# Eight start distances for the squared activations of a two-layer MLP

## The chip, the cores and the metric

The kernel runs on one core of a Trainium2 chip. The metric is the device time of one launch in microseconds: before the change the median of three runs is 565.23 us (563.58 to 565.45).

## The reference, cut to what matters

The program is a trunk of two decoder layers over 256 tokens of width 1024, all in fp32. Each layer has a token mixer with a memory cross-attention beside it, and then an MLP. The change touches only the MLP:

```python
D_MODEL, SEQ, DEPTH, D_FF = 1024, 256, 2, 4096

for i in range(DEPTH):
    # pooling mixer (layer 0) or block attention (layer 1), memory attention, w_out
    x = x + jnp.concatenate([tok, mo], axis=-1) @ w_out[i]
    u = rms_norm(x, g_mlp[i])
    x = x + jnp.square(jax.nn.relu(u @ w_ff1[i])) @ w_ff2[i]
return x
```

## The kernel before, in words

Every matrix product is made in a shortened fp32 form. An operand is split into a high part `hi` and a remainder `lo` (`split`, L105 to L115; ScalarE makes `hi`, VectorE makes `lo`), and a product is the sum of hi by hi, hi by lo and lo by hi. `mm3` (L117 to L120) issues these three multiplies into one PSUM tile. In a multiply TensorE holds one operand of 128 rows by 128 columns still (the weight load, PEld in the profile) and streams the other past it.

The MLP works in eight groups of 512 hidden features (`mlp`, L391 to L471).

- `ff1(g)` computes the group's hidden values. Here the split weights stand still, in pieces of 128 columns, and the transposed residual stream (`x1T`, in layer 1 `x3T`) is streamed: L418 streams 512 columns (high and low part side by side), L420 streams 256. The first group works in four accumulators and alternates four multiplies of L418 with four of L420; the other groups run eight and eight.
- `square` (L394 to L405) takes the result out of PSUM, applies the squared ReLU, and writes the split result: ScalarE writes `hh` at L404, VectorE writes `hl` at L405. Two such pairs a group hold four blocks of 128 features by 256 tokens.
- `ff2(g)` multiplies them into four accumulators. Here `hh` and `hl` stand still, in slices of 128 columns, and the split weights `hi` and `lo`, which came from HBM a moment ago, are streamed with 512 columns. That is 48 multiplies a group, 384 a layer, 768 in all.

The groups are interleaved: `ff1(g)` is issued, then `ff2(g - 1)`. The order on TensorE is the order of the code. All weights arrive over SyncE's DMA queue (L100).

Where a tile lies in SBUF is set by its pool. The pools of the weights (`rawp`, `wp`) and of the transposed activations (`tp`) hold tiles of whole multiples of 512 bytes a partition; in the program as built they all begin at 32 modulo 512. The pool `m0` of the first MLP and `m1` of the second, with `hh` and `hl`, begin behind the pool `mkp`, in which a tile that nothing uses takes 96 floats:

```python
    mkp.tile([P, 96], F32, tag="gap", name="gap")
```

With it `hh`, `hl` and the other tiles of `m0` and `m1` begin at 32 modulo 512 too. A slice of 128 fp32 columns is 512 bytes. So the start of a standing slice in `ff2` lies a whole multiple of 512 bytes from the start of the streamed weights. The same holds for `ff1`, `w_out` and the input projections.

Two places of layer 0 differ. The buffers `hhi` and `hlo` of the pooling stage follow a tile of 2304 bytes (`bw1`, L523), which is four and a half times 512, so they begin at 288. The band multiplies (L564, L565) hold slices of `hhi` and `hlo` and stream `bw0`, which begins at 32: a distance of 256. The keys of the memory attention of layer 0 (`mkh`, `mkl`, streamed) also begin at 288 and the queries (`mqh`, `mql`, standing) at 32; in layer 1 both begin at 32.

Of the kernel before, what the change touches and what calls it, by code (L numbers as in the profile page):

```python
# [11 lines left out]
F32R = mybir.dt.float32r  # L12
# [6 lines left out]
P = 128  # L19
# [14 lines left out]
QG, KG = 58, 122  # L34
NSMALL = 186
NWARM = 8
LAG = 2

PLAN = {'x': 6, 'q': 5, 'bw': 7, 'pool': 5, 'mem0': (1, 3, 6, 6),
# [14 lines left out]
def trunk(ctx: ExitStack, tc: tile.TileContext, x, mem, x_t, mem_t, small, bands, rope, mask,  # L54
# [13 lines left out]
    def nm(s):  # L68
        uid[0] += 1
        return f"{s}_{uid[0]}"  # L70

    def psum(name="ps"):
        return psp.tile([P, 512], F32, tag="ps", name=nm(name))

    def accum():
        return accp.tile([P, 512], F32, tag="acc", name=nm("acc"))
# [12 lines left out]
    wps = psum("warm")  # L89
    for _ in range(NWARM):  # L90
        nc.tensor.matmul(wps, warm[:, :P], warm, start=True, stop=True)
# [3 lines left out]
    def load_raw(src):  # L95

        n = src.shape[1]
        k = src.shape[0] // P
        r = rawp.tile([P, k, n], F32, tag="raw", name=nm("raw"))
        nc.sync.dma_start(r, src.rearrange("(k p) n -> p k n", p=P))  # L100
        return r
# [3 lines left out]
    def split(raw, g=None):  # L105
        n = raw.shape[-1]
        hi = wp.tile([P, n], F32R, tag="hi", name=nm("hi"))
        lo = wp.tile([P, n], F32R, tag="lo", name=nm("lo"))
        if g is None:
            nc.scalar.activation(hi, raw, AF.Copy)  # L110
            nc.vector.tensor_tensor(lo, raw, hi.bitcast(F32), op=ALU.subtract)  # L111
        else:
            last_hi[0] = nc.scalar.activation(hi, raw, AF.Copy, scale=g)  # L113
            nc.vector.scalar_tensor_tensor(lo, raw, g, hi.bitcast(F32), op0=ALU.mult, op1=ALU.subtract)  # L114
        return hi, lo  # L115

    def mm3(o, a, b, start, stop):  # L117
        nc.tensor.matmul(o, a[0], b[0], start=start, stop=False)  # L118
        nc.tensor.matmul(o, a[0], b[1], start=False, stop=False)  # L119
        nc.tensor.matmul(o, a[1], b[0], start=False, stop=stop)  # L120
# [20 lines left out]
    def big_t(name):  # L141

        t = tp.tile([P, NKC, 2, S], F32R, tag="t", name=nm(name))
        return t[:, :, 0, :], t[:, :, 1, :], t
# [125 lines left out]
    def later(fn):  # L270
        pend.append(fn)
        while len(pend) > LAG:
            pend.pop(0)()
# [108 lines left out]
    def mlp_stats():  # L382
        e2 = []
        for b in range(2):
            ms = norm_stats(xr[:, b, :], f"mlp{b}")
            r2 = st.tile([P, 1], F32, tag=f"r2{b}", name=nm("r2"))
            nc.vector.reciprocal(r2, ms)
            e2.append(r2)
        return e2

    def mlp(l, t, hp, finish):  # L391
        acc = []

        def square(zs, hh, hl):  # L394

            z = hp.tile([P, 2, S], F32, tag="r", name=nm("r"), bufs=2)
            for i in range(2):
                c = hp.tile([P, S], F32, tag="c", name=nm("c"), bufs=2)
                nc.scalar.activation(c, zs[i][:, S:], AF.Copy)  # L399
                nc.vector.tensor_tensor(z[:, i, :], zs[i][:, :S], c, op=ALU.add)  # L400
            z = z.rearrange("p i t -> p (i t)")
            h = hp.tile([P, 512], F32, tag="h", name=nm("h"), bufs=2)
            nc.vector.scalar_tensor_tensor(h, z, 0.0, z, op0=ALU.max, op1=ALU.mult)
            nc.scalar.activation(hh, h, AF.Copy)  # L404
            nc.vector.tensor_tensor(hl, h, hh.bitcast(F32), op=ALU.subtract)  # L405

        def ff1(g):
            pieces = []
            for q in range(4):
                raw = load_raw(w_ff1[l][q * 256:(q + 1) * 256, g * 512:(g + 1) * 512])  # L410
                for j in range(2):
                    k = 2 * q + j
                    pieces.append(split(raw[:, j, :], sm[:, GMLP + 8 * l + k:GMLP + 8 * l + k + 1]))

            def steps(o, n, ks):

                for k in ks:
                    nc.tensor.matmul(o, pieces[k][0][:, n * P:(n + 1) * P], t[2][:, k, :, :], start=k == 0, stop=False)  # L418
                for k in ks:
                    nc.tensor.matmul(o[:, :S], pieces[k][1][:, n * P:(n + 1) * P], t[0][:, k, :],  # L420
                                     start=False, stop=k == NKC - 1)

            res = [(hp.tile([P, 512], F32R, tag="hh", name=nm("hh"), bufs=4),
                    hp.tile([P, 512], F32R, tag="hl", name=nm("hl"), bufs=4)) for _ in range(2)]
            if g == 0:
                z = [accum() for _ in range(4)]
                for k0 in (0, 4):
                    for n in range(4):
                        steps(z[n], n, range(k0, k0 + 4))
                for i in range(2):  # L430
                    square(z[2 * i:2 * i + 2], *res[i])
                return res
            for i in range(2):
                z = [psum("step") for _ in range(2)]
                for n in range(2):
                    steps(z[n], 2 * i + n, range(NKC))
                square(z, *res[i])
            return res

        def ff2(g, hs):  # L440
            last = g == 7
            if g == 0:
                acc.extend([[accum(), accum()], [accum(), accum()]])
            held = []

            def go(b, h, f, pieces):
                hh, hl = hs[f // 2]
                o = (f % 2) * S + b * P
                mm3(acc[b][h], (hh[:, o:o + P], hl[:, o:o + P]), pieces[h], g == 0 and f == 0, last and f == 3)

            for f in range(4):
                raw = load_raw(w_ff2[l][g * 512 + f * P:g * 512 + (f + 1) * P, :])
                held.append([split(raw[:, 0, h * 512:(h + 1) * 512]) for h in range(2)])
                if not last:
                    for b in range(2):
                        for h in range(2):
                            go(b, h, f, held[f])
            if last:
                for h in range(2):
                    for b in range(2):  # L460
                        for f in range(4):
                            go(b, h, f, held[f])
                        finish(b, h, acc[b][h])

        prev = ff1(0)
        r2.extend(mlp_stats())
        for g in range(1, 8):
            cur = ff1(g)
            ff2(g - 1, prev)
            prev = cur  # L470
        ff2(7, prev)  # L471
# [11 lines left out]
    with tc.tile_pool(name="l0", bufs=1) as lp:  # L483
# [74 lines left out]
        dhi, dlo, _ = big_t("d")  # L558
# [59 lines left out]
        for l in range(2):  # L618
            g = cp.tile([P, 1], F32, tag=f"mg{l}", name=f"mg{l}")
# [45 lines left out]
    with tc.tile_pool(name="l1", bufs=1) as lp:  # L665
# [6 lines left out]
        for i, (gc, f) in enumerate(((QG, 1.0), (KG, 8.0))):  # L672
            for b in range(2):
                cc, ss = rp[:, b, 0, :], rp[:, b, 1, :]
                g1, g2 = sm[:, gc:gc + 32], sm[:, gc + 32:gc + 64]
                for j, (g, src, sg) in enumerate(((g1, cc, f), (g2, cc, f), (g2, ss, -f), (g1, ss, f))):
                    nc.vector.scalar_tensor_tensor(tcs[:, b, j // 2, i, (j % 2) * 32:(j % 2) * 32 + 32],
                                                   g, sg, src, op0=ALU.mult, op1=ALU.mult)
# [185 lines left out]
```

## Time and profile before

| | |
|---|---|
| median of three runs | 565.23 us (563.58 to 565.45) |
| profiled execution | 565.1 us, its span 563.3 us |
| TensorE (PE) busy | 554.2 us, 98% of the span |
| weight loads (PEld) busy | 459.6 us, 82% |
| VectorE (DVE) busy | 397.3 us, 71% |
| ScalarE (ACT) busy | 343.3 us, 61% |
| granted TensorE clock | 0.997 of full speed |
| moved by DMA | 101.94 MB, mean 181 GB/s |

The span reaches from the first to the last instruction. Multiplies are pipelined: the recorded duration of one reaches from its start until its last results are out, so that consecutive ones overlap, and what each takes of TensorE's time is read from the start of one to the start of the next. In the lists of groups a mean duration stands behind the busy time.

### The profile page before, as it was taken

The page shows a single profiled execution, that of the slowest core. Times are in us where ns is not written, and L with a number is a line of the kernel's source. Part 1 is how long each engine was busy: PE and PEld are TensorE (multiplying, and loading weights), DVE is VectorE, ACT ScalarE, POOL GpSimd, SP SyncE. Part 2 cuts the span into 40 slices and gives each one's busy share as a digit, 9 for nine tenths or more (in the row PEclk, how much of TensorE's full clock was granted, in tenths as well). Part 3 has the DMA queues.
Part 4 walks back from the last instruction along what each step waited for, and adds up shares of the span by engine and source line. Part 5 has one row for each costly group of instructions (what it writes and reads, how often), then busy time and mean ns, then how long its engine had stood idle before and what let it go on. Part 6 is the DMA issues. An engine that isn't in the chain of part 4 may idle for free.

```text
span 563.3 us, 8161 instructions
## 1 busy us (share of the span) xinstructions
PE 554.2 (98%) x2884; PEld 459.6 (82%) x2884; DVE 397.3 (71%) x793; ACT 343.3 (61%) x659; POOL 24.4 (4%) x27
## 2 busy tenths in 40 slices
PE   7999999999999999999999999999999999999997
PEld 3888788888888888888887777878888888888885
DVE  4798986775855856847879999667768477486542
ACT  5789976663763754745766887656647456466330
POOL 0111110000000000000012112000000000000000
PEclk9999999999999999999999999999999999999999
DMA  8979855546637548448563333455374483573301
GB/s 262 339 274 317 260 182 163 161 138 224 207 135 257 166 149 284 124 175 274 152 217 119 113 118 115 143 159 176 107 269 139 161 287 106 205 229 138 121 0 74
DMA packets 46696, 101.94 MB, mean 181 GB/s; under 512 B 3648, under 2 KB 11584, under 8 KB 46656
## 3 DMA queue, kind: packets, MB, share of 16 engines
q1 hardware_dynamic: 46656, 101.43, 54.9%
q8 instruction: 22, 0.36, 0.3%
q14 instruction: 18, 0.15, 0.1%
HBM read 100.37 MB, written 1.05 MB: 180 GB/s over the span
## 4 chain that ended last, share of the span: by engine, by line
PE 90%; DVE 3%; ACT 2%; DMA 1%; POOL 1%; issue 1%; SPq 0%; DVEq 0%; ACTq 0%
PE step L418 18%; PE acc L119 18%; PE acc L120 17%; PE acc L118 17%; PE step L420 9%; PE acc L418 3%; PE av_out L334 1%; PE acc L420 1%; DMA raw<-in_w_in_pool_dram 1%; PE exp_t L298 1%; POOL r L164 1%; PE transpose L137 1%; DVE lo L114 1%; PE tok_scores L714 1%; ACT hi L113 1%
## 5 line engine op out<-in xcount | busy, mean ns | idle before, releaser
L114 DVE SCALAR_TENSOR_TENSOR lo<-raw,sm,hi 128x512 fp32r<-128x512 f32 x212 | 150.5, 745 | 33.1 <-ACT hi L113 19.6
L113 ACT ACTIVATE hi<-raw,sm 128x512 fp32r<-128x512 f32 x212 | 140.8, 717 | 33.0 <-PE acc L120 29.9
L110 ACT ACTIVATE hi<-raw 128x512 fp32r<-128x512 f32 (+1 forms) x152 | 92.0, 626 | 46.1 <-PE acc L120 40.7
L111 DVE TENSOR_TENSOR lo<-raw,hi 128x512 fp32r<-128x512 f32 (+1 forms) x152 | 97.0, 682 | 19.7 <-ACT hi L110 19.7
L118 PE MATMUL acc<-hi,hh 128*128 128x512 f32 x256 | 99.9, 390 | 0.0
L119 PE MATMUL acc<-lo,hh 128*128 128x512 f32 x256 | 99.8, 390 | 0.0
L120 PE MATMUL acc<-hi,hl 128*128 128x512 f32 x256 | 99.8, 390 | 0.0
L400 DVE TENSOR_TENSOR r<-step,c 128x256 f32<-128x256 f32 x56 | 23.6, 422 | 57.8 <-ACT c L399 57.8
L399 ACT ACTIVATE c<-step 128x256 f32<-128x256 f32 x56 | 21.3, 380 | 68.8 <-PE step L420 68.8
L120 PEld LDWEIGHTS acc<-hi,hl 128*128 128x128 f32 x256 | 48.1, 188 | 10.1
L418 PE MATMUL step<-x1T,hi 128*128 128x512 f32 x224 | 55.9, 392 | 0.0
L418 PE MATMUL step<-x3T,hi 128*128 128x512 f32 x224 | 55.9, 392 | 0.0
L118 PEld LDWEIGHTS acc<-hi,hh 128*128 128x128 f32 x256 | 48.1, 188 | 9.5
L119 PEld LDWEIGHTS acc<-lo,hh 128*128 128x128 f32 x256 | 48.1, 188 | 9.4
L418 PEld LDWEIGHTS step<-x3T,hi 128*128 128x128 f32 x224 | 40.7, 189 | 7.5
L418 PEld LDWEIGHTS step<-x1T,hi 128*128 128x128 f32 x224 | 40.6, 189 | 7.5
L420 PEld LDWEIGHTS step<-x3T,lo 128*128 128x128 f32 x224 | 30.6, 190 | 2.2
L420 PEld LDWEIGHTS step<-x1T,lo 128*128 128x128 f32 x224 | 30.6, 190 | 2.2
L118 PE MATMUL acc<-hi,x2T 128*128 128x512 f32 x80 | 32.1, 401 | 0.0
L120 PE MATMUL acc<-hi,x2T 128*128 128x512 f32 x80 | 31.7, 396 | 0.0
L119 PE MATMUL acc<-lo,x2T 128*128 128x512 f32 x80 | 31.6, 395 | 0.0
L420 PE MATMUL step<-x3T,lo 128*128 128x256 f32 x224 | 31.2, 282 | 0.0
(148 smaller groups left out, 775.9 us busy)
## 6 DMA issues: line engine op xcount, KB each, us to landing
raw<-in_w_ff_dram SPq DMA_DIRECT2D x128, 512.0 KB, 4.6
raw<-in_w_out_dram SPq DMA_DIRECT2D x16, 512.0 KB, 4.5
raw<-in_w_in_moba_dram SPq DMA_DIRECT2D x24, 256.0 KB, 4.2
raw<-in_w_mem_kv_dram SPq DMA_DIRECT2D x8, 512.0 KB, 5.2
raw<-in_w_in_moba_dram SPq DMA_DIRECT2D x8, 512.0 KB, 4.9
raw<-in_w_in_pool_dram SPq DMA_DIRECT2D x7, 512.0 KB, 7.0
xr<-in_x_dram SPq DMA_DIRECT2D x2, 512.0 KB, 8.2
raw<-in_mem_t_dram SPq DMA_DIRECT2D x4, 256.0 KB, 6.9
```

The costliest lines, as they stand in the source:

```text
L110: nc.scalar.activation(hi, raw, AF.Copy)
L111: nc.vector.tensor_tensor(lo, raw, hi.bitcast(F32), op=ALU.subtract)
L113: last_hi[0] = nc.scalar.activation(hi, raw, AF.Copy, scale=g)
L114: nc.vector.scalar_tensor_tensor(lo, raw, g, hi.bitcast(F32), op0=ALU.mult, op1=ALU.subtract)
L118: nc.tensor.matmul(o, a[0], b[0], start=start, stop=False)
L119: nc.tensor.matmul(o, a[0], b[1], start=False, stop=False)
L120: nc.tensor.matmul(o, a[1], b[0], start=False, stop=stop)
L137: nc.tensor.transpose(ps[:, c * P:(c + 1) * P], src[:, (c0 + c) * P:(c0 + c + 1) * P], ident)
L399: nc.scalar.activation(c, zs[i][:, S:], AF.Copy)
L400: nc.vector.tensor_tensor(z[:, i, :], zs[i][:, :S], c, op=ALU.add)
L418: nc.tensor.matmul(o, pieces[k][0][:, n * P:(n + 1) * P], t[2][:, k, :, :], start=k == 0, stop=False)
L420: nc.tensor.matmul(o[:, :S], pieces[k][1][:, n * P:(n + 1) * P], t[0][:, k, :], start=False, stop=k == NKC - 1)
```

## The change

```diff
+RES = (256, 384, 64, 32, 192, 320, 448, 96)
...
-            res = [(hp.tile([P, 512], F32R, tag="hh", name=nm("hh"), bufs=4),
-                    hp.tile([P, 512], F32R, tag="hl", name=nm("hl"), bufs=4)) for _ in range(2)]
+            res = []
+            for i in range(2):
+                j = 2 * (g % 2) + i
+                u = hp.tile([P, 9 * P], F32R, tag=f"hb{j}", name=nm("hb"), bufs=1)
+                o = RES[4 * l + j] // 4
+                res.append((u[:, o:o + 512], u[:, o + 512:o + 1024]))
```

`hh` and `hl` of a pair now lie in one tile `hb` of 1152 floats, one behind the other, and begin `RES` bytes behind its start. There are four such tiles a layer (`hb0` and `hb1` for the even groups, `hb2` and `hb3` for the odd ones), each with a single buffer; before, there were four buffers of `hh` and four of `hl`, used in turn. A tile is 4608 bytes a partition, nine times 512, and in the program as built all four begin at 32 modulo 512. So the distance between standing and streamed operand in `ff2`, modulo 512, is the number in `RES`: 256, 384, 64 and 32 in layer 0, 192, 320, 448 and 96 in layer 1, each for 96 of the 768 multiplies. The pool grows by 2048 bytes a partition, and its other tiles (`r`, `c`, `h`, `o`) move by multiples of 32.

No instruction moves. Both programs have 5153 instructions, which stand in the same order on every engine and wait for the same semaphores at the same values. Line numbers behind the new constant rise by two, those behind the new loop by six: `mm3` is L119 to L122 in the changed kernel, L418 and L420 become L420 and L422.

## Rows read from the trace of the kernel before

**Rows 1.** The page: part 1's TensorE line, and part 4's chain by engine.
```profile
PE 554.2 (98%) x2884; PEld 459.6 (82%) x2884; DVE 397.3 (71%) x793; ACT 343.3 (61%) x659; POOL 24.4 (4%) x27
...
PE 90%; DVE 3%; ACT 2%; DMA 1%; POOL 1%; issue 1%; SPq 0%; DVEq 0%; ACTq 0%
```
**Rows 2.** Busy time by stretch: us, each engine, granted clock, DMA share, GB/s.
```profile
120.00:285.00 165.00, 165.00 (x827) 139.99 (x826) 115.52 (x204) 95.56 (x170) 1.12 (x2) 1.00 0.59 194
...
392.00:563.30 171.30, 167.41 (x846) 142.49 (x844) 105.36 (x175) 84.54 (x154) 0.00 (x0) 1.00 0.46 155
```
**Rows 3.** Groups of instructions: shapes, count | busy us, mean ns | idle before.
```profile
L118 PE MATMUL acc<-hi,hh 128*128 128x512 f32 x256 | 99.9, 390 | 0.0
L119 PE MATMUL acc<-lo,hh 128*128 128x512 f32 x256 | 99.8, 390 | 0.0
L120 PE MATMUL acc<-hi,hl 128*128 128x512 f32 x256 | 99.8, 390 | 0.0
L418 PE MATMUL step<-x1T,hi 128*128 128x512 f32 x224 | 55.9, 392 | 0.0
...
L403 DVE SCALAR_TENSOR_TENSOR h<-r 128x512 f32<-128x512 f32 x32 | 22.0, 688 | 0.5
L405 DVE TENSOR_TENSOR hl<-h,hh 128x512 fp32r<-128x512 f32 x32 | 22.0, 687 | 9.9 <-ACT hh L404 9.8
...
L404 ACT ACTIVATE hh<-h 128x512 fp32r<-128x512 f32 x32 | 20.0, 626 | 17.6 <-DVE h L403 17.6
...
L418 PE MATMUL acc<-x1T,hi 128*128 128x512 f32 x32 | 8.7, 394 | 0.0
```
**Rows 4.** Timeline of TensorE at the start of one ff2 group: start us, us.
```profile
208.57 0.40 PE L118 MATMUL acc<-hi,hh 128*128 128x512 f32 x1
208.81 0.40 PE L119 MATMUL acc<-lo,hh 128*128 128x512 f32 x1
209.04 0.39 PE L120 MATMUL acc<-hi,hl 128*128 128x512 f32 x1
209.27 0.40 PE L118 MATMUL acc<-hi,hh 128*128 128x512 f32 x1
209.50 0.39 PE L119 MATMUL acc<-lo,hh 128*128 128x512 f32 x1
209.74 0.39 PE L120 MATMUL acc<-hi,hl 128*128 128x512 f32 x1
209.96 0.39 PE L118 MATMUL acc<-hi,hh 128*128 128x512 f32 x1
...
212.00 0.39 PE L118 MATMUL acc<-hi,hh 128*128 128x512 f32 x1
```
**Rows 5.** Instructions of the tile hh: count, duration min/median/max in ns.
```profile
L118 PE MATMUL acc<-hi,hh x256: 387/389/478, 120.4 to 558.6; 128*128 128x512 f32 x128
```
**Rows 6.** The same of the tile x1T, first group of layer 0.
```profile
L418 PE MATMUL acc<-x1T,hi x32: 387/396/401, 97.5 to 108.5; 128*128 128x512 f32 x32
```
**Rows 7.** Groups on TensorE, 32.7 to 34.0 us, of the pooling bands.
```profile
L564 PE MATMUL band<-bw,hhi 128*128 128x512 f32 x2 | 0.7, 394 | 0.0
...
L565 PE MATMUL band<-bw,hlo 128*128 128x512 f32 x1 | 0.4, 397 | 0.0
```
**Rows 8.** Timeline of TensorE, memory scores of layer 0.
```profile
69.35 0.38 PE L118 MATMUL mem_scores<-mkh,mqh 64*128 64x256 f32 x1
69.57 0.28 PE L119 MATMUL mem_scores<-mkl,mqh 64*128 64x256 f32 x1
...
70.04 0.28 PE L120 MATMUL mem_scores<-mkh,mql 64*128 64x256 f32 x1
```
**Rows 9.** Timeline of TensorE, memory scores of layer 1.
```profile
311.13 0.38 PE L118 MATMUL mem_scores<-mkh,mqh 64*128 64x256 f32 x1
311.36 0.28 PE L119 MATMUL mem_scores<-mkl,mqh 64*128 64x256 f32 x1
...
311.83 0.28 PE L120 MATMUL mem_scores<-mkh,mql 64*128 64x256 f32 x1
```

## The prediction

> **What bounds the kernel now.** I read the page first, then the busy time by stretch, then the groups of instructions, and last single starts on TensorE's timeline. The page has TensorE busy for 554.2 of 563.3 us and 90% of the chain that ended last on it [rows 1]. The stretches say that this is no average over unlike stages where the change acts: from 120 to 285 us, which holds all eight ff2 groups of layer 0 and a little of layer 1's projections, TensorE is busy for 165.00 of 165.00 us, and from 392 us to the end, which holds those of layer 1, for 167.41 of 171.30 us, at a granted clock of 1.00 [rows 2]. So in the MLP the end is set by the pace of the multiplies. Whatever one multiply of ff2 gains or loses reaches the end at its full size, since nothing else is late there. With 768 such multiplies, 1 ns on each is 0.77 us.
>
> The pace itself is in the starts. In the ff2 group that begins at 208.57 us the first six intervals take 209.96 - 208.57 = 1.39 us, 232 ns each, and the next nine 212.00 - 209.96 = 2.04 us, 227 ns each [rows 4]. The recorded duration falls with the interval, from 0.40 us for the first two to 0.39 us from the fifth on. So the means of the groups can be read as paces: ff2's three lines have a mean of 390 ns [rows 3] with a median of 389 and a lowest of 387 [rows 5], so nearly all run at the settled pace of 227 ns. The first group of ff1 changes its kind of multiply every four and has a mean of 394 [rows 3], median 396, highest 401 [rows 6]: it never settles. The settled pace is thus a state that a run of like multiplies falls into after about six, and that a change of rhythm breaks.
>
> **The change part by part.** Instructions, their order and their waits are the same, so no wait is added and none removed, and nothing is moved past a queue. That hh and hl now share a tile costs nothing for the same reason: the multiplies wait for the same signals. What changes are addresses.
>
> *Writing the buffers.* L404 (626 ns) and L405 (687 ns) write, and L403 (688 ns) and L405 read, at other multiples of 32 bytes, 32 times each [rows 3]. I take no cost. If each of the 96 became 10% longer, that would be 32 x (63 + 69 + 69) = 6.4 us of ScalarE and VectorE, which lies beside TensorE: a pair is first read by TensorE a whole ff1 group after it is made, and TensorE has no idle time before any ff2 multiply [rows 3]. Without that cover the price would be that 6.4 us; I keep it out of the range, since in the MLP of layer 0 the two engines are busy for 115.52 and 95.56 of 165 us [rows 2].
>
> *The 768 multiplies.* While one multiply streams its 512 columns, the next one's 128 columns are loaded. Before, both reads begin a multiple of 512 bytes apart in all of ff1 and ff2. Afterwards they begin at eight other distances. No long run of 512 columns with another distance stands in this trace, so the cost is bounded by what is near.
>
> - From below: the shortest recorded ff2 duration is 387 ns, 3 under the mean [rows 5], so 768 x 3 = 2.3 us gained, 562.8 us. Farther off, 512 columns at 2.4 GHz, the level that a clock of 1.00 stands for, take 213 ns, 14 under the settled 227 [rows 4]: at most 768 x 14 = 10.8 us, 554.3 us. Nothing in the trace runs at that pace.
> - From above: the three band multiplies of 512 columns at a distance of 256, in the one stretch where they follow each other, record 394 ns (the mean of two) and 397 ns [rows 7], against 390 for ff2. At 397 it would be 768 x 7 = 5.4 us, 570.5 us; at 401, the slowest unsettled multiply [rows 6], 768 x 11 = 8.4 us, 573.5 us.
> - In between: multiplies that never settle have a mean of 394 [rows 3]. That is 4 ns each, 3.1 us if all eight distances do that, 568.2 us.
>
> I take the middle bound as the price, because it is the nearest row (same stage, same shape, same operands' sizes, another rhythm) and the band rows begin at the same figure. And I take it for five of the eight distances, as a choice between none and all: 768 x 5/8 x 4 ns = 1.9 us. The profiled execution took 565.1 us (span 563.3 us and 1.8 us around it), 0.1 us under the median of the runs shown, so the two need no correction: 565.1 + 1.9 = **567.0 us**.
>
> Why a loss at all, when the sign of an address effect isn't known? Because ff2 already sits near the bottom of what 512-column multiplies do here: 3 ns lie between its mean and its lowest, 7 to 11 between its mean and the values of the unsettled ones. If the distance has a part in the settling, a scattered set of distances has more room to lose than to win.
>
> One pair of rows speaks against a loss: the memory scores of the two layers, at distances of 256 and 0, take the same 0.47 us for four starts [rows 8, 9]. The Trainium skill has a rule for that: TensorE: Matmul & The Clock Gate, section "Step-by-step: what each phase is for", says that the array has two independent SBUF read ports, one for the streamed operand and one for the weights, and that loading the next tile's weights takes no read bandwidth from the running multiply. By it the sum is nil and the time 565.1 us. For that pair of rows the trace agrees.
>
> **The rivals.** *The distance has a hold on the pace* is the forecast, and can cost from one distance of eight (0.4 us) to all eight at 397 ns (5.4 us).
>
> *No effect.* The settling comes from the rhythm of multiplies alone, and ff2 keeps 227 ns. Time: 565.1 us, within 0.3% like any value from 563.5 to 566.9 us. For it speaks the only like-for-like pair of the trace. The memory scores of layer 0 run at a distance of 256, those of layer 1 at 0. The first start-to-start is 0.22 us in the one [rows 8] and 0.23 us in the other [rows 9]; the next four take 70.04 - 69.57 = 0.47 us and 311.83 - 311.36 = 0.47 us. And the band rows are beginnings: ff2 starts a group just as slowly at distance 0 [rows 4]. Against it: these runs are six multiplies long with 256 columns, too short to show where a run settles, and 256 is one distance of eight.
>
> *Faster.* The settled 227 ns hold 14 ns above the 213 ns of streaming. If those come from both reads starting at the same place modulo 512, other distances shorten them. A quarter of it, or the lowest recorded pace, is about 3 ns each, 2.3 us: 562.8 us. It counts as faster from 2.1 ns on. For it: all stages with the settled pace have distance 0, so its cause can't be told apart from the distance. Against it: the layer 0 scores at 256 are no shorter. The Trainium skill (TensorE: Matmul & The Clock Gate, "Back-to-back issue gap") gives 512/2.4 + 2.5, about 216 ns, for a warm multiply; by that figure the gain would be, as an estimate, 768 x 11 ns, and no row here shows that pace.
>
> *The change does nothing to the distance* I leave out: each new tile begins at 32 modulo 512 as the weights do, so the distances are those of the table.
>
> **How the numbers follow.** Against the median of 565.23 us a difference of 0.3%, 1.7 us or 2.2 ns a multiply, is about what a measurement of this kernel can tell from no change. Forecast (the distance costs): 0.47, of which 0.40 lies above 566.9 us and 0.07 below. No effect: 0.34. Faster: 0.19, of which 0.17 lies below 563.5 us and 0.02 above. So faster 0.17, same 0.07 + 0.34 + 0.02 = 0.43, slower 0.40. The likeliest case's own range is 565.5 to 570.5 us. The range is 562.3 to 570.5 us: the upper end is all multiplies at 397 ns, and the lower end is half a microsecond below the lowest pace seen; I leave about 0.08 below and 0.08 above.
>
> **What the changed profile would show.** The three lines of mm3 with the tiles of `hb` tell it at once: a mean near 390 ns and a median of 389 is no effect, 392 to 397 the forecast, 388 or less the gain. Group by group the four tiles of a layer must differ if the distance counts: inside a stretch of 24 multiplies on one tile the starts are 227 ns apart at a good distance, and stay at 231 to 236 ns at a bad one. L420 and L422 of ff1 should keep 392 ns, with their first multiplies after ff2 perhaps less settled. The forecast is wrong if all eight tiles keep 227 ns, if the pace changes where no `hb` tile is read, or if the time grows by waits before multiplies instead of by their pace.

## The result and the profile after

The changed kernel takes 566.97 us (median of 7 runs, 566.57 to 568.51), the kernel before 564.72 us in the same comparison (7 runs, 563.56 to 565.45). The ratio is 1.0054, 95% interval 1.0040 to 1.0067: slower, and the whole interval lies above the 0.3% that the prediction took for no change.

The page of the changed kernel, part 1 and the groups of the ff2 multiplies and of ff1's first kind (count | busy us, mean ns of one | idle before):

```profile
PE 556.1 (98%) x2884; PEld 459.2 (81%) x2884; DVE 397.6 (70%) x793; ACT 344.0 (61%) x659; POOL 24.5 (4%) x27
...
L122 PE MATMUL acc<-hi,hb 128*128 128x512 f32 x256 | 101.1, 395 | 0.0
L121 PE MATMUL acc<-lo,hb 128*128 128x512 f32 x256 | 100.9, 394 | 0.0
L120 PE MATMUL acc<-hi,hb 128*128 128x512 f32 x256 | 100.7, 393 | 0.0
...
L420 PE MATMUL step<-x1T,hi 128*128 128x512 f32 x224 | 56.0, 392 | 0.0
```

Where ff2's three lines had a mean of 390 ns [rows 3], they have 393 to 395. Their busy time rises from 99.9 + 99.8 + 99.8 to 302.7 us, by 3.2 us. ff1's line keeps 392. The median of the tile, 389 ns before [rows 5], is now 394 (count, min/median/max, first and last start):

```profile
L120 PE MATMUL acc<-hi,hb x256: 388/394/477, 118.9 to 560.5; 128*128 128x512 f32 x128
```

From the first to the last ff2 multiply 441.6 us pass, against 558.6 - 120.4 = 438.2 us before [rows 5]: 3.4 us more. That is more than the 2.0 us between the two spans, since this execution came to its first ff2 multiply 1.5 us sooner. The difference arose at 11 to 15 us, where TensorE's clock was down in the profiled execution of the kernel before. The stretch from 11 to 15 us in the kernel before, and then in the changed one (busy us and count of PE, PEld, DVE, ACT, POOL; granted clock; DMA share; GB/s):

```profile
11.00:15.00 4.00, 3.95 (x10) 2.86 (x11) 4.00 (x8) 3.34 (x6) 0.00 (x0) 0.58 1.05 389
```

```profile
11.00:15.00 4.00, 3.94 (x16) 2.98 (x17) 4.00 (x8) 3.37 (x6) 0.00 (x0) 1.00 1.05 390
```

A mean of 0.58 says that most of the stretch ran at the lower of the two levels, 1.2 GHz: 10 multiplies in place of 16. TensorE had waited for ScalarE just before in both, 1.79 and 1.87 us, so that wait alone does not decide. Of the profiled executions this one (565.1 us) and e10 below (564.98 us, 0.57 in the same stretch) have the clock down there, and e1 (563.0 us, 1.00) does not. The mean granted clock of a run parts the kernel before in the same way: of 54 more runs of it, made beside the experiments, the 29 at 0.998 or more take 562.83 to 563.85 us and the 25 at 0.997 or less 564.47 to 565.41 us. Of the changed kernel six of seven runs are at 0.999 or more, between 566.57 and 567.04 us, and the seventh, at 0.997, takes 568.51 us. At the full clock (0.998 or more, here and below) the change costs about 3.5 us, 566.9 against 563.4 us; the medians show less because five of the seven runs of the kernel before, by their times, had the clock fall.

The pace breaks on the timeline at the border between the first tile (distance 256) and the second (384) of the first group of the changed kernel (start us, us of one):

```profile
122.07 0.39 PE L122 MATMUL acc<-hi,hb 128*128 128x512 f32 x1
...
123.88 0.39 PE L121 MATMUL acc<-lo,hb 128*128 128x512 f32 x1
124.11 0.40 PE L122 MATMUL acc<-hi,hb 128*128 128x512 f32 x1
124.34 0.40 PE L120 MATMUL acc<-hi,hb 128*128 128x512 f32 x1
124.58 0.40 PE L121 MATMUL acc<-lo,hb 128*128 128x512 f32 x1
124.82 0.39 PE L122 MATMUL acc<-hi,hb 128*128 128x512 f32 x1
125.05 0.39 PE L120 MATMUL acc<-hi,hb 128*128 128x512 f32 x1
...
125.97 0.40 PE L121 MATMUL acc<-lo,hb 128*128 128x512 f32 x1
...
129.70 0.40 PE L122 MATMUL acc<-hi,hb 128*128 128x512 f32 x1
```

From 122.07 to 123.88 eight intervals take 226 ns each, the settled pace. From 124.34 to 129.70 the 23 intervals on the second tile take 233 ns each, and they don't come down.

### The profile page after: what moved, and what is told of

Its sections match the earlier page's. It is cut to its first block, busy times and chain, and to the rows that moved or that the text cites. A ratio compares the mean times of both kernels' runs of the same rounds, so it can differ in the third digit from the quotient of the medians.

```text
span 565.3 us, 8161 instructions
## 1 busy us (share of the span) xinstructions
PE 556.1 (98%) x2884; PEld 459.2 (81%) x2884; DVE 397.6 (70%) x793; ACT 344.0 (61%) x659; POOL 24.5 (4%) x27
## 4 chain that ended last, share of the span: by engine, by line
PE 90%; DVE 3%; ACT 2%; DMA 1%; POOL 1%; issue 1%; SPq 0%; DVEq 0%; ACTq 0%
PE step L420 18%; PE acc L121 18%; PE acc L122 17%; PE acc L120 17%; PE step L422 9%; PE acc L420 3%; PE av_out L336 1%; PE acc L422 1%; DMA raw<-in_w_in_pool_dram 1%; PE exp_t L300 1%; POOL r L166 1%; PE transpose L139 1%; DVE lo L116 1%; PE tok_scores L720 1%; ACT hi L115 1%
## 5 line engine op out<-in xcount | busy, mean ns | idle before, releaser
L122 PE MATMUL acc<-hi,hb 128*128 128x512 f32 x256 | 101.1, 395 | 0.0
L121 PE MATMUL acc<-lo,hb 128*128 128x512 f32 x256 | 100.9, 394 | 0.0
L120 PE MATMUL acc<-hi,hb 128*128 128x512 f32 x256 | 100.7, 393 | 0.0
L122 PEld LDWEIGHTS acc<-hi,hb 128*128 128x128 f32 x256 | 48.1, 188 | 10.9
L121 PEld LDWEIGHTS acc<-lo,hb 128*128 128x128 f32 x256 | 48.1, 188 | 10.7
L120 PEld LDWEIGHTS acc<-hi,hb 128*128 128x128 f32 x256 | 48.1, 188 | 10.5
L420 PE MATMUL step<-x3T,hi 128*128 128x512 f32 x224 | 56.0, 392 | 0.0
L420 PE MATMUL step<-x1T,hi 128*128 128x512 f32 x224 | 56.0, 392 | 0.0
L420 PEld LDWEIGHTS step<-x3T,hi 128*128 128x128 f32 x224 | 40.7, 189 | 7.7
L420 PEld LDWEIGHTS step<-x1T,hi 128*128 128x128 f32 x224 | 40.7, 189 | 7.7
L422 PEld LDWEIGHTS step<-x3T,lo 128*128 128x128 f32 x224 | 30.6, 190 | 2.2
L422 PEld LDWEIGHTS step<-x1T,lo 128*128 128x128 f32 x224 | 30.5, 190 | 2.2
L122 PE MATMUL acc<-hi,x2T 128*128 128x512 f32 x80 | 31.7, 396 | 0.0
L121 PE MATMUL acc<-lo,x2T 128*128 128x512 f32 x80 | 31.6, 395 | 0.0
L422 PE MATMUL step<-x3T,lo 128*128 128x256 f32 x224 | 31.2, 282 | 0.0
```

## The experiments

The theory: the distance modulo 512 between the slice that is loaded next and the operand that is streamed sets the pace, and nothing else of the change counts. The rivals: the new tile layout costs; the absolute start of the standing slice counts, not the distance; the loss comes from eight distances following each other; each distance has one pace of its own, whatever ran before.

**The layout alone (e1) and one distance alone (e2).** Both change only the table:

```diff
-RES = (256, 384, 64, 32, 192, 320, 448, 96)
+RES = (0,) * 8      # e1
+RES = (32,) * 8     # e2
```

> The changed kernel with all eight distances set to 0, everything else of the change kept (one tile for a pair, four single buffers, r, c, h and o moved). If the distance is the cause, the three lines of the ff2 multiplies go back to a mean of 390 ns and the time to that of the kernel before, within 0.3%. If the new tiles or the moved neighbours are the cause, the lines stay at 393 to 395 ns and the time at about 567 us.

> All eight distances set to 32. If each distance has a pace of its own, all 768 multiplies run like those that had 32 in the changed kernel, about 396 ns, 6 to 7 ns over the kernel before: 768 x 6.5 ns = 5 us more than before, about 570 us. If the loss came from the distances changing every 24 multiplies and so breaking the settled rhythm, one distance throughout settles again: 390 to 391 ns and 565 us.

Measured: e1 takes 563.37 us (10 runs) beside 563.61 us of the kernel before (13 runs), ratio 0.9998 (0.9983 to 1.0012). Its groups:

```profile
L120 PE MATMUL acc<-hi,hb 128*128 128x512 f32 x256 | 99.9, 390 | 0.0
L121 PE MATMUL acc<-lo,hb 128*128 128x512 f32 x256 | 99.8, 390 | 0.0
L122 PE MATMUL acc<-hi,hb 128*128 128x512 f32 x256 | 99.8, 390 | 0.0
```

e2 takes 567.94 us (4 runs), ratio 1.0071 (1.0056 to 1.0087), 4.3 us by the medians where 5 were expected; all four are at the full clock, where the difference is 4.6 us. Its groups:

```profile
L120 PE MATMUL acc<-hi,hb 128*128 128x512 f32 x256 | 101.4, 396 | 0.0
L122 PE MATMUL acc<-hi,hb 128*128 128x512 f32 x256 | 101.3, 396 | 0.0
L121 PE MATMUL acc<-lo,hb 128*128 128x512 f32 x256 | 101.2, 395 | 0.0
```

The tiles, the single buffers and the moved neighbours cost nothing. One distance throughout does not settle again, so it isn't the alternation that costs.

**The place or the distance (e5).** Eight floats ahead of all tiles:

```diff
+    cp.tile([P, 8], F32, tag="pad", name="pad")
     xr = cp.tile([P, 2, D], F32, tag="xr", name="xr")
-RES = (256, 384, 64, 32, 192, 320, 448, 96)
+RES = (0,) * 8
```

> Distance 0 throughout, but 8 floats ahead of all tiles, so that streamed and standing operands all begin at 64 modulo 512 instead of 32. If only the distance counts, ff2's three lines keep 390 ns and starts 227 ns apart. If the absolute start of the standing slice counts, they change as they did for the tile with 32 more in the changed kernel, to about 395 ns (some 4 us more).

One execution took 563.25 us, with ff2 at 390 ns and everything at 64 modulo 512 (its `mm3` is L121 to L123):

```profile
L121 PE MATMUL acc<-hi,hb 128*128 128x512 f32 x256 | 99.9, 390 | 0.0
...
L123 PE MATMUL acc<-hi,hb 128*128 128x512 f32 x256 | 99.8, 390 | 0.0
L122 PE MATMUL acc<-lo,hb 128*128 128x512 f32 x256 | 99.8, 390 | 0.0
```

In the changed kernel a standing slice at 64 beside weights at 32 ran off the settled pace (the tile with distance 32); here a slice at 64 beside weights at 64 settles. So it is the distance, not the place. At a distance other than 0 the place was not moved.

**A table of distances (e3, e6).** The rest of the multiples of 32, and finer steps:

```diff
+RES = (128, 160, 224, 288, 352, 416, 480, 16)   # e3
+RES = (4, 8, 12, 20, 24, 28, 240, 272)          # e6
```

> Eight distances not tried so far: 128, 160, 224, 288 in layer 0, 352, 416, 480 and 16 in layer 1. A look at the pace of each. If the pace follows from the distance smoothly, 224 and 288 lie between those of 192, 256 and 320 (starts 227 to 233 ns apart), and 128, 160, 352, 416 and 480 at 229 to 234 ns. None is expected under 226 ns; one that is would be of use for a faster kernel. If the pace is set by the absolute start of the standing slice, the same values are expected, so this run does not tell those two apart.

> Distances that are no multiple of 32: 4, 8, 12, 20 in layer 0, 24, 28, 240, 272 in layer 1. So far 0, 16 and 256 settle at 227 ns and 32, 224 and 288 at 233. If the good places are a band from 0 up to somewhere between 16 and 32 and repeat every 256 bytes, then 4, 8, 12 and 272 settle at 227, 20 to 28 show where the band ends, and 240 tells whether it reaches below 256. If the pace depends on the distance without such a band (each distance its own), values between 226 and 241 come in no order.

One execution each: 568.56 and 566.44 us. For the table, starts were taken from the traces: the mean interval over the 24 multiplies of a tile, in the groups where one tile follows the other (the last group of a layer takes them in turn and is left out), and the intervals that repeat inside a tile.

| distance | ns, mean | intervals, ns | distance + 256 | ns, mean |
|---|---|---|---|---|
| 0 | 227.8 | 227, after a slow start | 256 | 227.8 |
| 32 | 233.4 | 235, 232 | 288 | 233.3 |
| 64 | 233.3 | 231, 236 | 320 | 233.3 |
| 96 | 234.2 | 231, 238, 237, 231, 234, 235, 234 | 352 | 233.9 |
| 128 | 232.4 | 241, 232, 231, 232, 228, 230, 232 | 384 | 232.9 |
| 160 | 233.0 | 237, 231, 232 | 416 | 233.7 |
| 192 | 229.0 | 226, 229, 232 | 448 | 228.9 |
| 224 | 233.1 | 231, 235, 233, 234 | 480 | 233.2 |

(0 and 256 are the first tiles of a group in e1 and e10; the second tiles have 226.7. The intervals are those of the left column. Most of the right column repeats the same ones; 320 does not, it goes through 233, 233 and 234.) The finer steps: 4 has 232.0, 8 has 230.7, 12 has 230.0 (224 and 236 in turn), 20 has 233.2, 24 has 231.0, 28 has 234.9, 240 has 229.0, 272 has 232.9 ns. No band around 0 leads to the settled pace: behind ff1's 256-column multiplies even a distance of 4 does not reach it, so this expectation was wrong. None of the finer steps was run behind a settled tile, so whether one of them would hold the pace there is not shown. And the smooth course expected in e3 isn't there either: 224 and 288 lie beside 256 and are as slow as the rest. But d and d + 256 agree within 0.7 ns, five of the eight pairs within 0.1.

**Is it modulo 256 (e10)?**

```diff
+RES = (256,) * 8
```

> All eight distances at 256. In the runs so far the distances d and d + 256 went through the same intervals (64 and 320, 128 and 384, 192 and 448, 160 and 416), and 256 like 0. If the rule is modulo 256, this kernel runs like the one before: 390 ns on the three lines, 227 ns settled, time within 0.3%. If 512 is the modulus, ff2 differs from 390 ns.

Measured: 563.63 us (10 runs) beside 563.64 us (13 runs), ratio 1.0000 (0.9986 to 1.0015), the three lines at 390 ns:

```profile
L120 PE MATMUL acc<-hi,hb 128*128 128x512 f32 x256 | 99.9, 390 | 0.0
L122 PE MATMUL acc<-hi,hb 128*128 128x512 f32 x256 | 99.8, 390 | 0.0
L121 PE MATMUL acc<-lo,hb 128*128 128x512 f32 x256 | 99.8, 390 | 0.0
```

At a grain of 32 bytes the rule is modulo 256. Of the pairs that the expectation names, 64 and 320 share the mean and not the intervals. The step of 16 fits in too: 272 in e6 goes through 233, 233, 234, 231, 234 and 235 ns, the intervals of 16 in e8 below.

**One distance, two paces (e8, e9).** In e3 the tile with 16 stood at 227 ns, which made 16 look as good as 0, or better.

```diff
+RES = (16,) * 8                         # e8
+RES = (0, 16, 0, 16, 16, 0, 16, 0)      # e9
```

> All eight distances at 16. In the run with 16 on one tile its 24 multiplies stood at 227 ns from the first on, but it was never the first tile of a group. If a distance of 16 also does away with the slow start of a group (233, 236, 228, 232, 231 ns at distance 0), ff2 wins 16 x 25 ns = 0.4 us against distance 0, to about 389.5 ns a multiply; the time is that of the kernel before within 0.1%. If 16 only works once the pace is settled, the first tile of a group runs at 230 ns and more and ff2 loses 1 to 2 us.

> Layer 0: the first tile of each group at distance 0, the second at 16. Layer 1: the first at 16, the second at 0. With 16 throughout, the multiplies stood at 232 to 235 ns, but behind a tile at 480 one tile with 16 ran at 227. If the pace is a state that a run is in and that a distance can hold without leading into it, layer 0's tiles with 16 start from the settled 227 and keep it, and layer 1's, which follow ff1's 256-column multiplies, run at 233: the lines with hb then have means of 390 in layer 0 and about 393 in layer 1. If each distance has one pace, 16 costs the same in both layers.

e8 takes 569.07 us (6 runs) beside 564.6 us, ratio 1.0081 (1.0062 to 1.0100); I had expected no loss, or 1 to 2 us. Its groups:

```profile
L121 PE MATMUL acc<-lo,hb 128*128 128x512 f32 x256 | 101.7, 397 | 0.0
L122 PE MATMUL acc<-hi,hb 128*128 128x512 f32 x256 | 101.3, 396 | 0.0
L120 PE MATMUL acc<-hi,hb 128*128 128x512 f32 x256 | 100.9, 394 | 0.0
```

e9 (one execution, 565.06 us) shows that 16 has two paces. The starts of the tiles in the first group of layer 0, distance 0 and then 16, and of layer 1, 16 and then 0:

```profile
119.19 0.40 PE L120 MATMUL acc<-hi,hb 128*128 128x512 f32 x1
...
124.66 0.39 PE L120 MATMUL acc<-hi,hb 128*128 128x512 f32 x1
...
130.09 0.39 PE L420 MATMUL step<-x1T,hi 128*128 128x512 f32 x1
...
404.01 0.39 PE L120 MATMUL acc<-hi,hb 128*128 128x512 f32 x1
...
409.61 0.40 PE L120 MATMUL acc<-hi,hb 128*128 128x512 f32 x1
...
415.07 0.39 PE L420 MATMUL step<-x3T,hi 128*128 128x512 f32 x1
```

In layer 0 the 24 multiplies at 16 take 130.09 - 124.66 = 5.43 us, 226 ns each; in layer 1 those at 16 take 409.61 - 404.01 = 5.60 us, 233 ns each. The same distance has two paces, and what ran before decides which one holds. It is not simply the pace before: in e3 the tile with 16 came behind one with 480 that was itself off the settled pace. The starts of these two and of the multiply behind them:

```profile
429.10 0.39 PE L120 MATMUL acc<-hi,hb 128*128 128x512 f32 x1
...
434.69 0.39 PE L120 MATMUL acc<-hi,hb 128*128 128x512 f32 x1
...
440.13 0.39 PE L420 MATMUL step<-x3T,hi 128*128 128x512 f32 x1
```

The 24 multiplies at 480 take 434.69 - 429.10 = 5.59 us, 233 ns each, and those at 16 then 440.13 - 434.69 = 5.44 us, 227 ns each. What in the multiplies before sets 16 on one or the other is not shown, and most distances of the table were run behind one predecessor only, so they may have a second pace as well. Distance 0 leads to 227 ns from any start that was seen: in layer 1 it settles behind a tile at 233.

**Which multiply pays (e4).**

```diff
+RES = (0,) * 8
-                res.append((u[:, o:o + 512], u[:, o + 512:o + 1024]))
+                res.append((u[:, o:o + 512], u[:, o + 520:o + 1032]))
```

> Distance 0 for all hh, 32 for all hl (8 floats of room between the two). It tells which multiply pays: if it is the one that streams while the next one's weights are loaded, the middle line of mm3 pays (its successor loads hl): about 396 ns there, 390 on the other two. If it is the one whose own weights lie at the distance, the last line pays (it holds hl): 396 there, 390 on the others. If the pace is a state of the run as a whole, all three rise to about 392. Time 768 / 3 x 6 ns = 1.5 us over the kernel before in the first two cases.

One execution took 567.81 us, 4.2 us over the median of the kernel before (563.61 us), where 1.5 us were expected. Its groups:

```profile
L121 PE MATMUL acc<-lo,hb 128*128 128x512 f32 x256 | 102.1, 399 | 0.0
L120 PE MATMUL acc<-hi,hb 128*128 128x512 f32 x256 | 101.3, 396 | 0.0
L122 PE MATMUL acc<-hi,hb 128*128 128x512 f32 x256 | 99.9, 390 | 0.0
```

The middle line, which streams while hl is loaded, pays most, and the last line, which holds hl and streams while a slice at 0 is loaded, pays nothing by its duration. That agrees with the next load beside the running stream. But the first line, which has nothing to do with hl, pays 6 ns too, and from start to start the three lines repeat at 232, 239 and 229 ns, where all three stand at 226.7 once settled. So none of the three expectations held alone: a disturbance goes on into later multiplies. By the sum of ff2's intervals one load in three at a bad distance costs 4.4 us against e1, and all three in e2 cost 4.5 us.

**Other stages (e7).** The transposed activations moved by 32 bytes, ff2 left at 0:

```diff
+    tp.tile([P, 8], F32, tag="pad", name="pad", bufs=1)
-    mkp.tile([P, 96], F32, tag="gap", name="gap")
+    mkp.tile([P, 88], F32, tag="gap", name="gap")
+RES = (0,) * 8
```

> Distance 0 in ff2, but the transposed activations (all tiles of the pool tp) moved by 32 bytes against the weights. So the roles are others: in ff1 the weights stand and the activations are streamed, at a distance of 480 in 512 multiplies of 512 columns and 512 of 256; in the input projections and w_out the activations stand and the weights are streamed at 32, in some 500 multiplies. If the rule holds wherever a weight load runs beside a stream, ff1's L420 rises from 392 to about 396 ns and the projections by as much where they don't wait: 1000 x 4 to 6 ns = 4 to 6 us more than before, 569 to 571 us, with ff2 at 390 ns. If it is a matter of the hb tiles, all stays at 390 and 392 ns and the time at that of before within 0.3%.

Measured: 568.39 us (5 runs) beside 563.64 us, ratio 1.0064 (1.0044 to 1.0084): 4.75 us more by the medians. Three of the five runs had the clock fall; at the full clock it is 566.9 against 563.4 us, 3.4 us more, a little under the 4 to 6 us of the rule. ff1 and one line of the input projections in the kernel before, and then in this one, where ff1 is L422 and L424:

```profile
L418 PE MATMUL step<-x1T,hi 128*128 128x512 f32 x224 | 55.9, 392 | 0.0
...
L118 PE MATMUL acc<-hi,x2T 128*128 128x512 f32 x80 | 32.1, 401 | 0.0
...
L420 PE MATMUL step<-x1T,lo 128*128 128x256 f32 x224 | 31.2, 282 | 0.0
```

```profile
L422 PE MATMUL step<-x1T,hi 128*128 128x512 f32 x224 | 56.8, 395 | 0.0
...
L120 PE MATMUL acc<-hi,x2T 128*128 128x512 f32 x80 | 32.4, 405 | 0.0
...
L424 PE MATMUL step<-x1T,lo 128*128 128x256 f32 x224 | 30.8, 280 | 0.0
```

ff1's 512-column line rises from 392 to 395 ns, and in the projections, with the roles exchanged, the line of hi and x2T rises from 401 to 405, and the other two lines of mm3 there by 4 and 5 ns. The expectation had not reckoned with the 256-column line of ff1, which came down from 282 to 280 ns: from start to start 117.3 in place of 119.0 ns, 0.8 us in all, which is part of why the loss stayed under 4 us. So 480, which is bad for one length, is a little better for another.

**A version that gains (e11).** No distance tried beats the settled 227 ns, so the table holds no faster kernel. What the starts at distance 0 do show is a slow beginning of the 512-column multiplies each time they follow those of 256. The edit is made in the kernel before, with its distances of 0; `part` 0 issues the 512-column multiplies of a feature block (L418) and `part` 1 those of 256 (L420):

```diff
-                for n in range(2):
-                    steps(z[n], 2 * i + n, range(NKC))
+                for part in range(2):
+                    for n in range(2):
+                        steps(z[n], 2 * i + n, range(NKC), part)
```

> The kernel before, with all its distances at 0, but in the groups 1 to 7 of ff1 the multiplies of a pair of feature blocks stand in another order: sixteen of 512 columns and then sixteen of 256, in place of eight, eight, eight, eight. Nothing else is changed. At distance 0 a stretch of 512-column multiplies begins with 233, 236, 228, 232, 231 ns when it follows 256-column ones, 25 ns more than settled. If that slow start comes from the change of rhythm, two of the four in a group go: 28 x 25 ns = 0.7 us in all, L418 falls from 392 to about 390.5 ns, the time by 0.1%. If the slow start comes with each new PSUM tile or each new set of weights, L418 keeps 392 ns.

Measured: 562.88 us (12 runs) beside 563.75 us (17 runs), ratio 0.9983 (0.9971 to 0.9996).

```profile
L418 PE MATMUL step<-x1T,hi 128*128 128x512 f32 x224 | 53.3, 390 | 0.0
```

L418 falls from 392 to 390 ns. The gain is small, 0.9 us by the medians and 0.7 us at the full clock (9 and 10 runs), with 0.7 expected, but a ratio of 1 lies outside the interval. From start to start L418 falls from 229.4 to 227.6 ns, 0.8 us in all, and L420 rises from 119.0 to 119.5, 0.2 us: a stretch of 256-column multiplies begins with a short interval (113 or 114 ns) before it comes to 120, and there are fewer such beginnings now. The busy time of L418 falls further, from 55.9 to 53.3 us, because longer runs of one group overlap more of their own durations; of that column only the mean is comparable.

## Why the prediction came out right, step by step

*The bound.* Right. TensorE was the bound in both MLPs, and the loss came whole: 3.2 us more busy time in ff2, 3.4 us more from its first to its last multiply.

*No cost from the new tiles and the moved neighbours.* Right: e1.

*A settled pace that a disturbance breaks, with ff2 near its bottom.* Right, and more so than the argument had it. That the distance has a part in the settling was a guess, as the prediction says itself with its "if": no row of the kernel before shows it. With distances of 0 or 256 ff2 settles; with most others it falls into a short cycle of intervals that repeats for as long as the tile lasts.

*Five of the eight distances lose, at 4 ns each.* The count was a choice between none and all that no row supported, and that it came out is luck: 384, 64, 32, 320 and 96 stand at 233 to 234 ns. 256 loses nothing, and 192 and 448 lose about 1 ns against the 227.8 of a first tile. The 4 ns were the mis-sized term. The five stand 6 to 8 ns over the settled 226.7, since they never settle at all, while the unsettled rows that gave the price [rows 3, 6] settle in part (their lowest, 387 ns, is ff2's lowest too). So ff2 costs 3.2 us, not 1.9. That the median still came out at the predicted 567.0 us is in part luck: 3.2 us on a profiled execution of 565.1 would be 568.3, and what brought it back are the 1.5 us at 11 to 15 us, which that execution had lost at the lower clock and most runs of the changed kernel did not. The upper end of the range, from band rows at a distance of 256, rested on nothing that this distance does: a long run at 256 settles (e10), and those rows are slow as beginnings, as the prediction says under its rival.

*The rival with no effect* rested on the memory scores at distances of 256 and 0 [rows 8, 9]. The reading was right and its reach was not: 256 is the one distance of the eight that acts like 0. A single pair of distances was no test of the others. The Trainium skill's rule that a weight load takes no read bandwidth from the running multiply (TensorE: Matmul & The Clock Gate, "Step-by-step: what each phase is for") would have ff2 keep its pace at every distance. Here the measured pace departs from the settled 226.7 ns by up to 8 ns (at a distance of 28, e6), and the measurement decides.

*The faster rival* fell: distances other than 0 don't shorten the 227 ns. Nothing tried has a mean below 226.7.

What stays open is the mechanism. The runs show that the distance modulo 256 and, at 16, what ran before decide the pace, and e4 points to the next load beside the running stream. No run looks into the memory, so what collides there is not shown. Nor is it shown which waits more, the load or the stream.

## What to carry to other kernels

On a stage where TensorE is the bound, and each multiply of 512 fp32 columns has a load of its own as here, lay the standing and the streamed operand a whole multiple of 256 bytes apart, counted from the start of the slice that is loaded to the start of the operand that is streamed, and check it after any tile of odd size is added to a pool: here 4 bytes off cost 4 ns in 228, and 32 bytes 6. Keep like multiplies in long runs: going from 256 to 512 columns costs some 25 ns here and going back returns some 7, so that e11 won 40 ns in each group of ff1 by leaving out two of its four rounds. And read the pace from start to start on a stretch of like multiplies, at both of its ends: a pace belongs to a run and not to one instruction, so a short run in an old trace says little about a long one in a new kernel.

## What was unexpected of the hardware

The intervals form fixed cycles of up to seven multiplies, the same in every group that runs the distance: 231 and 236 at 64, 226, 229 and 232 at 192 and 448, 224 and 236 at 12. At 16 two states exist, 227 and 233 ns, and what ran before picks one (e9, and e3 behind 480). And the rule has a period of 256 bytes, half the length of the slice.
